# Loading a stage's weights from GpSimd's DMA queue in a hybrid attention and state space kernel

## The chip, the cores and the metric

The kernel runs on one core of a Trainium2 chip. The metric is the device time of one execution in microseconds. TensorE (PE) multiplies, VectorE (DVE) and ScalarE (ACT) work elementwise, GpSimd (POOL) does a few small operations, and SyncE (SP) does nothing but issue DMA transfers. ScalarE issues some transfers too. Each engine works through its own row of instructions in order.

## The reference

One step of a two-layer streaming encoder for 256 new frames of one stream and 32 frames of another, 288 columns in all, with a model width of 2048. Layer 0 is attention. Layer 1, which the change touches, is a state space layer:

```
h, gate = adaln(x, c, ...)
u, z = split(h @ w_in_ssm, 2)                  # 2048 x 4096
y, state = s5_sequence(u, state, abar, bbar, c)  # diagonal complex recurrence
y = y + d * u
g = gelu(y)
glu = g * sigmoid(g @ w_glu + b_glu)
x = x + gate * ((glu * silu(z)) @ w_out_ssm)
```

The recurrence has 128 groups of 16 channels with a complex state of 64 each. All values are float32.

## The kernel before, in words

Activations lie transposed, channels on partitions, as 16 tiles of 128 x 288. A weight matrix is cut into jobs: one job is one load of 1 MB (128 x 4 x 512) and the matmuls on it. To keep float32 precision, ScalarE rounds each quarter of a weight tile to `hi`, VectorE computes `lo` = w - hi, and TensorE multiplies hi and lo with a likewise split activation (`ah`, `al`): three matmuls, called a triple here, for each 128 x 128 block. One job has 16 triples. `w_in_ssm` has 32 jobs: the first 16 make u in four groups of four tiles, the other 16 make z.

Weight tiles lie in slots. `pump` (line 391) loads the next job's weights as soon as a slot is free, and a slot is free when the last `lo` of its tile is done. There are four slots; in the state space stage one of them is given to UL, so three serve the weights. The loads are written on SyncE, so a load whose slot is not free yet waits there, and all that is behind it in SyncE's row waits too.

The recurrence is side work beside the main stream, written by Python generators:

- `state_in` (line 1612): when a group of four u tiles is finished, it writes them to HBM (`ud<-MX`, one DMA) and reads them back with time steps on partitions (`MX<-ud`, eight DMAs, short pieces). Then TensorE makes `xin_ps` for each tile with weights that ScalarE loads.
- `lags` (line 1592): reads lagged copies of u (`UL<-ud`, four DMAs for a tile) into two buffers in turn.
- `inside` (line 1728): `t_ps` from UL and a small weight `kb`; then VectorE adds it to u. When t_ps is through, its UL buffer is free for the tile after next.
- `scan` (line 1651): VectorE's recurrence over 32 steps, 16 columns of two groups at a time.
- `slices` (line 1693): ScalarE arranges the states in `Xm`, TensorE makes `y_ps` with a loaded `v`; after four tiles the result goes to HBM (`yd<-Yg`, eight DMAs, short pieces).
- `gelus` (line 1750): reads it back (`yx<-yd`), adds it and applies GELU; `act_split` then makes the chunks of g.

A batch below is one round of this for four tiles; there are four.

The order of all this is fixed when the program is built. `Plan` keeps a time for each engine, `Engine.cost` (line 134) adds a cost for each instruction, and a generator goes on when the plan says that what it waits for is there. For a DMA from SyncE or GpSimd the plan has one common clock, `p.at["dma"]`, on which transfers queue one after the other. For a DMA from ScalarE it has a fixed latency and twice the size, without a queue. The written order of each engine comes from these numbers; what happens on the chip is decided by semaphores. Nearly all instructions go through line 116, so the profile is read by tiles and not by lines.

`rstd1` in `ready` marks the point early in layer 1 at which the norm of its input is there.

Of the kernel before, what the change touches and what calls it, by code (L numbers as in the profile page):

```python
# [38 lines left out]
class Plan:  # L39
# [35 lines left out]
    def run(self, eng, cost, outs, ins):  # L75
        t = self.at[eng]
        for a in ins:
            t = max(t, self.when(self.written, a) + self.LINK[eng])
        for a in outs:
            t = max(t, self.base.get(a.tensor.name, 0.0), self.when(self.read, a))  # L80
            if eng != "pe":
                t = max(t, self.when(self.written, a))
        self.at[eng] = t + cost
        end = t + cost + (0.07 if eng == "pe" else 0.0)
        for a in ins:
            self.note(self.read, a, end)
        for a in outs:
            self.note(self.written, a, end)
        self.last = max(self.last, end)
        return end  # L90
# [5 lines left out]
class Engine:  # L96
# [38 lines left out]
    def cost(self, fn, out, ins, outs, k):  # L135
        p = self.plan
        n = 1
        for d in out.shape[1:]:
            n *= d
        if fn == "dma_start":  # L140
            t = max([p.when(p.written, a) for a in ins] + [p.at[self.name], p.base.get(out.tensor.name, 0.0)])
            p.at[self.name] = t + (0.45 if self.name != "pool" else 1.0)
            size = self.pieces(out, ins[0])
            if self.name == "act":
                end = t + 3.2 + 2 * size
            else:
                p.at["dma"] = max(p.at["dma"], t + 1.2) + size
                end = p.at["dma"] + 2.0
            p.note(p.written, out, end)
            for a in ins:  # L150
                p.note(p.read, a, end)
            p.last = max(p.last, end)
            return
        if self.name == "pe":
            r = ins[1] if len(ins) > 1 else ins[0]
            w = 1
            for d in r.shape[1:]:
                w *= d
            m = out.shape[0]
            c = 0.107 if fn != "matmul" else w * 0.00042 + 0.01 if r.dtype == F32R else max(w * 0.00042, 0.024) if m <= 32 \  # L160
                else max(w * 0.00168, m * 0.00167)
            c += 0.003
        elif self.name == "act":
            c = n * 0.000833 + 0.1 + (0.1 if len(outs) > 1 else 0)
        elif self.name == "dve":
            if fn == "tensor_reduce":
                n = ins[0].shape[1] * (ins[0].shape[2] if len(ins[0].shape) > 2 else 1)
            c = 0.07 + n * (0.0063 if fn == "reciprocal" else 0.00055 if fn in ("tensor_copy", "memset") or fn == "tensor_scalar" and len(ins) < 2 else 0.00105)
        else:
            c = 0.14 + n * (0.166 if k.get("op") == ALU.pow else 0.0009 if fn == "tensor_scalar" else 0.0021)  # L170
        p.run(self.name, c, outs, ins)
# [100 lines left out]
def build(tc, I, O):  # L272
    nc = tc.nc
    plan = Plan()
    pe, act, dve, pool, sp = (Engine(e, n, plan) for e, n in (
        (nc.tensor, "pe"), (nc.scalar, "act"), (nc.vector, "dve"), (nc.gpsimd, "pool"), (nc.sync, "sp")))
# [4 lines left out]
    with ExitStack() as ctx:  # L281
# [12 lines left out]
        ready = Keys(plan)  # L294
# [88 lines left out]


        jobs = []
        st_of = {}
        pos = dict(load=0, run=0)
        st_free, slot_of, taken = list(range(NST)), {}, []
        more = dict(tiles={}, until=0)

        def pump():
            while pos["load"] < len(jobs):
                k = pos["load"]
                j = jobs[k]
                if j["kind"] == "fn":
                    j["fn"]()
                else:
                    free = [s for s in st_free if s < NST or k < more["until"]]
                    if not free:
                        break  # L400
                    slot_of[k] = free[-1] if free[-1] >= NST else free[0]
                    st_free.remove(slot_of[k])
                    t = more["tiles"][slot_of[k]]() if slot_of[k] >= NST else \
                        wst.tile([128, 4, 512], F32, tag="w%d" % slot_of[k], name="w")
                    sp.dma_start(t, j["src"])
                    st_of[k] = t
                pos["load"] += 1

# [32 lines left out]
        def rest_step(left):  # L441

            while len(rests) > left:
                k, i, st, hi, lo = rests.pop(0)
                TT(lo, st[:, i, :], hi.bitcast(F32), ALU.subtract)
                if i == 3:
                    st_done(k)
                    pump()
# [28 lines left out]
        def run_jobs(upto, n_side):  # L477
            while pos["run"] < upto:
                t = pos["run"]
                j = jobs[t]  # L480
                pump()
                if j.get("before"):
                    j["before"]()
# [942 lines left out]


        pump()
        side.add(x_stats())
        side.add(params())  # L1430
# [351 lines left out]
        for gi in range(4):  # L1782
            g = new_group(z1_evac(gi))
            for c in range(4):
                jobs.append(main_job("w_in_ssm", 4 + gi, c, g, "h1"))
                if gi == 3:
                    jobs[-1]["key"] = ("free", "h1", c)
        l1b = len(jobs)

        def glu_evac(gi):  # L1790
            def ev(n, ps, c):
# [225 lines left out]
```

## Time and profile before

| what | value |
|---|---|
| median of 3 runs | 1371.33 us (1369.74 to 1377.06) |
| the profiled execution | 1372.13 us |
| its span, first to last instruction | 1369.6 us |
| PE busy | 1237.1 us, 90% |
| DVE busy | 922.6 us, 67% |
| ACT busy | 593.4 us, 43% |
| POOL busy | 32.6 us |
| HBM read and written | 307.13 MB and 35.95 MB, 250 GB/s over the span |
| mean granted clock of TensorE | 0.960 |

The state space layer's w_in_ssm and recurrence lie from about 740 to 1145 us; the side work of the recurrence begins at about 800 us. PE's busy share is high because matmuls overlap in the records, so the time is read from the idle stretches and from what ended them. "x <-DMA y" behind a PE row names the transfer whose landing ended the wait.

### The profile page before, as it was taken

How to read it: one execution, taken by the hardware profiler on the slowest of the kernel's cores; microseconds unless marked ns; L12 is line 12 of the kernel's file. 1: busy time of each engine (PE TensorE's matmuls, PEld its weight loads, DVE VectorE, ACT ScalarE, POOL GpSimd, SP SyncE). 2: the span in 40 equal slices, each digit the busy share in tenths (PEclk: the TensorE clock that was granted, in tenths of full speed). 3: DMA queues.
4: the chain of work that ended last, by engine and by line, in shares of the span. 5: the costliest groups of instructions: out<-in, count | busy, mean ns of one | idle time of the engine just before them, and what ended most of it. 6: DMA issues, size and time to landing. Idle time of an engine off the chain costs nothing.

```text
span 1369.6 us, 28062 instructions
## 1 busy us (share of the span) xinstructions
PE 1237.1 (90%) x11098; PEld 1098.7 (80%) x11098; DVE 922.6 (67%) x2210; ACT 593.4 (43%) x1394; POOL 32.6 (2%) x21
## 2 busy tenths in 40 slices
PE   5999899999898999998899997875997998999996
PEld 3788798888787878886789896764986998989895
DVE  4579978788777877884556953745944965455454
ACT  4533233343454454454443743321553484444341
POOL 0006000000000000000000000000000000000000
PEclk9999999999999999999899998987988999999998
DMA  9978676688878878878665697989499366777631
GB/s 360 372 299 321 233 283 252 232 289 327 308 277 292 314 270 305 308 251 337 231 251 182 210 298 201 236 218 222 150 186 254 132 200 243 262 263 264 245 124 70
DMA packets 125442, 344.90 MB, mean 252 GB/s; under 512 B 50784, under 2 KB 75376, under 8 KB 94592
## 3 DMA queue, kind: packets, MB, share of 16 engines
q1 hardware_dynamic: 112640, 313.47, 67.9%
q10 hardware_dynamic: 12672, 29.65, 5.9%
q8 instruction: 87, 1.43, 0.4%
q14 instruction: 43, 0.35, 0.1%
HBM read 307.13 MB, written 35.95 MB: 250 GB/s over the span
## 4 chain that ended last, share of the span: by engine, by line
issue 44%; PE 32%; DVE 11%; DMA 10%; ACT 2%; POOL 0%; ACTq 0%; SPq 0%; DVEq 0%; POOLq 0%
PE m L116 24%; PE mod_ps L116 4%; DMA w<-in_w_in_att 4%; DVE lo L116 2%; DMA w_d<-W 2%; DMA v_d<-v 2%; DVE v L116 2%; DVE MX L116 1%; DVE tmpv L116 1%; ACT hi L116 1%; PE w_ps L116 1%; DVE qkv L116 1%; DVE dtmp L116 1%; DMA Fb<-Fp_d 1%; DVE ssq L116 1%
## 5 line engine op out<-in xcount | busy, mean ns | idle before, releaser
L116 PE MATMUL m<-ah,hi 128*128 128x288 f32 (+1 forms) x2304 | 714.6, 310 | 13.3 <-ACT hi L116 4.8
L116 PE MATMUL m<-ah,lo 128*128 128x288 f32 (+1 forms) x2304 | 689.8, 299 | 4.3 <-DVE lo L116 4.3
L116 PE MATMUL m<-al,hi 128*128 128x288 f32 (+1 forms) x2304 | 690.7, 300 | 0.4 <-DVE al L116 0.4
L116 PEld LDWEIGHTS m<-ah,hi 128*128 128x128 f32 x2304 | 443.0, 192 | 69.7 <-issue 32.3
L116 DVE TENSOR_TENSOR lo<-w,hi 128x512 fp32r<-128x512 f32 x552 | 368.4, 686 | 169.0 <-ACT hi L116 164.5
L116 ACT CAST hi<-w 128x512 fp32r<-128x512 f32 x552 | 322.0, 617 | 325.0 <-PE m L116 203.3
L116 PEld LDWEIGHTS m<-ah,lo 128*128 128x128 f32 x2304 | 443.2, 192 | 6.2 <-DVE lo L116 6.1
L116 PEld LDWEIGHTS m<-al,hi 128*128 128x128 f32 x2304 | 443.6, 193 | 1.0 <-DVE al L116 0.8
L116 PE MATMUL mod_ps<-w,cs 128*32 128x512 f32 x744 | 97.6, 619 | 12.6 <-DVE ssq L116 12.6
L116 DVE SCALAR_TENSOR_TENSOR qkv<-m,qkv 128x288 f32<-128x288 f32 x168 | 73.0, 452 | 25.9 <-PE m L116 25.7
L116 DVE TENSOR_TENSOR X<-X,t 128x32 f32<-128x32 f32 (+1 forms) x256 | 58.3, 228 | 8.2
L116 DVE TENSOR_TENSOR v<-pt,raw 128x512 f32<-128x512 f32 (+1 forms) x64 | 46.0, 718 | 13.5 <-DMA v_d<-v 13.4
L116 DVE SCALAR_TENSOR_TENSOR MX<-MX,c_dT,t_ps 128x288 f32<-128x288 f32 x16 | 8.2, 512 | 68.5 <-PE t_ps L116 68.5
L116 PE MATMUL t_ps<-UL,kb 128*32 128x288 f32 (+1 forms) x256 | 18.8, 420 | 38.4 <-DMA UL<-ud 38.4
L116 DVE SCALAR_TENSOR_TENSOR MX<-m,gate,MX 128x256 f32<-128x256 f32 x96 | 30.8, 363 | 32.2 <-PE m L116 32.1
L116 PEld LDWEIGHTS mod_ps<-w,cs 128*32 128x32 f32 x744 | 17.2, 110 | 38.0 <-issue 22.2
L116 DVE TENSOR_TENSOR tmpv<-pt,raw 128x512 f32<-128x512 f32 (+1 forms) x64 | 45.9, 718 | 0.0
L116 PEld LDWEIGHTS t_ps<-UL,kb 128*32 128x32 f32 x256 | 8.4, 124 | 46.1 <-issue 42.7
L116 PE MATMUL y_ps<-Xm,v 128*128 128x74 f32 x256 | 34.7, 294 | 10.4 <-DMA v<-v_d 5.3
L116 PEld LDWEIGHTS y_ps<-Xm,v 128*128 128x128 f32 x256 | 33.4, 210 | 11.4 <-ACT Xm L116 6.0
L116 ACT ACTIVATE yx<-MX 128x288 f32<-128x288 f32 (+1 forms) x38 | 18.8, 495 | 50.7 <-DVE MX L116 50.2
L116 DVE TENSOR_TENSOR v<-v,tmpv 128x512 f32<-128x512 f32 (+1 forms) x48 | 34.3, 714 | 1.7
(226 smaller groups left out, 910.6 us busy)
## 6 DMA issues: line engine op xcount, KB each, us to landing
w<-in_w_mod SPq DMA_DIRECT2D x93, 1024.0 KB, 6.2
w<-in_w_in_att SPq DMA_DIRECT2D x40, 1024.0 KB, 7.5
w<-in_w_in_ssm SPq DMA_DIRECT2D x32, 1024.0 KB, 6.7
w<-in_w_wide SPq DMA_DIRECT2D x24, 1024.0 KB, 10.1
w<-in_w_out_att SPq DMA_DIRECT2D x16, 1024.0 KB, 7.0
w<-in_w_glu SPq DMA_DIRECT2D x14, 1024.0 KB, 6.8
w<-in_w_out_ssm SPq DMA_DIRECT2D x12, 1024.0 KB, 5.2
v_d<-v ACTq DMA_DIRECT2D x16, 576.0 KB, 8.3
```

The lines of the kernel that those rows point to most:

```text
L116: return f(*a, **k)
```

## The change

Weight loads of the jobs up to the end of w_in_ssm (`l1b`) that are written after `rstd1` is ready are issued from GpSimd's queue. All others stay on SyncE. In the plan, a DMA from GpSimd gets the formula that ScalarE's had, so the common clock is SyncE's alone.

```
-            if self.name == "act":
-                end = t + 3.2 + 2 * size
-            else:
+            if self.name == "sp":
                 p.at["dma"] = max(p.at["dma"], t + 1.2) + size
                 end = p.at["dma"] + 2.0
+            else:
+                end = t + 3.2 + 2 * size
...
         jobs = []
+        ends = {}
...
         def pump():
+            side_end = ends.get("l1b", 0)
...
-                    sp.dma_start(t, j["src"])
+                    (pool if "rstd1" in ready and k < side_end else sp).dma_start(t, j["src"])
...
-        l1b = len(jobs)
+        l1b = ends["l1b"] = len(jobs)
```

Since the plan's times change, the written order of the other engines changes as well. On SyncE at the start of the first batch, the order before has these rows (ud and MX<-ud are the write and the read back of u, UL the lagged copies in their two buffers, kb the small weights of t_ps, x1d a copy of x in HBM):

```order
L116 DMA w<-in_w_in_ssm 128x2048 x2
L116 DMA ud<-MX 128x4x288
L116 DMA w<-in_w_in_ssm 128x2048
L116 DMA MX<-ud 16x32x36 x8
L116 DMA UL<-ud 32x4x288 x4
L116 DMA UL_9942<-ud 32x4x288 x4
L116 DMA w<-in_w_in_ssm 128x2048 x2
L116 DMA kb<-kb_d 128x256
L116 DMA UL<-ud 32x4x288 x4
L116 DMA kb<-kb_d 128x256
L116 DMA UL_9942<-ud 32x4x288 x4
```

The same place has these rows now:

```order
L116 DMA x1d<-MX 128x1152 x2
L116 DMA ud<-MX 128x4x288
L116 DMA MX<-ud 16x32x36 x8
L116 DMA UL<-ud 32x4x288 x4
L116 DMA UL_9942<-ud 32x4x288 x4
L116 DMA kb<-kb_d 128x256
L116 DMA UL<-ud 32x4x288 x4
L116 DMA kb<-kb_d 128x256
L116 DMA UL_9942<-ud 32x4x288 x4
L116 DMA kb<-kb_d 128x256 x2
```

The weight loads ahead of ud, of MX<-ud and of the third set of UL are gone from SyncE's row; the rest keeps its sequence.

In the third batch SyncE has this order before (v are the weights of y_ps, yd the write of its result):

```order
L116 DMA UL<-ud 32x4x288 x4
L116 DMA v_11330<-v_d 128x1152
L116 DMA w<-in_w_in_ssm 128x2048
L116 DMA kb<-kb_d 128x256
L116 DMA UL_9942<-ud 32x4x288 x4
L116 DMA v_11391<-v_d 128x1152
L116 DMA yd<-Yg 16x32x36 x8
L116 DMA w<-in_w_in_ssm 128x2048
L116 DMA kb<-kb_d 128x256
L116 DMA UL<-ud 32x4x288 x4
```

And this one now:

```order
L116 DMA v_11374<-v_d 128x1152
L116 DMA MX<-ud 16x32x36 x8
L116 DMA UL<-ud 32x4x288 x4
L116 DMA UL_9942<-ud 32x4x288 x4
L116 DMA v_11443<-v_d 128x1152
L116 DMA yd<-Yg 16x32x36 x8
L116 DMA kb<-kb_d 128x256
L116 DMA UL<-ud 32x4x288 x4
L116 DMA kb<-kb_d 128x256
L116 DMA UL_9942<-ud 32x4x288 x4
```

The weights are gone here too, and the eight yd stand between the second and the third set of UL as before. GpSimd's row ends with these operations now (Xm is cleared by a memset; nrm is the small operation of a norm, the last one that of the final norm):

```order
L116 MEMSET SZ 128x1728
L116 MEMSET Xm 128x592
L116 TENSOR_TENSOR nrm<-nrm,mhalf 128x3
L116 DMA w<-in_w_in_ssm 128x2048 x26
L116 TENSOR_TENSOR nrm<-nrm,mhalf 128x3
```

Before, the two nrm stood next to each other; the 26 loads are what came between them.

In TensorE's order the instructions are the same in number. Counted in triples of w_in_ssm from its start, the first xin_ps of the four batches stood at 114, 184, 226 and 356 and stand at 106, 170, 236 and 300; a group of four u tiles ends at 64, 128, 192 and 256. In a batch xin_ps and t_ps now mostly alternate with two triples between one and the next. The last y_ps stood at 500 and stands at 416, and w_in_ssm ends at 512. Everything behind w_in_ssm has the order that it had.

## The prediction

> **What bounds the kernel now.** I read the page's granted clock by slices, then a table of windows over the state space stage, then TensorE's waits in it, then SyncE's issues in order of time, and last the DMA issues with their time to landing. The page first: the profiled execution has a span of 1369.6 us.
>
> ```profile
> PEclk9999999999999999999899998987988999999998
> ```
>
> The clock sags only between slices 24 and 31, which is the state space stage. The windows cut that stretch, 800 to 1145 us, into five parts (length, busy us of PE, PEld, DVE, ACT, POOL with their counts, clock, DMA share, GB/s).
>
> ```profile
> 800.00:848.00 48.00, 37.38 (x386) 33.29 (x385) 15.52 (x31) 17.09 (x45) 0.00 (x0) 0.89 0.84 224
> 848.00:905.00 57.00, 49.49 (x492) 46.16 (x491) 42.95 (x156) 23.47 (x61) 0.00 (x0) 0.97 0.93 234
> 905.00:959.00 54.00, 30.73 (x338) 26.36 (x331) 24.69 (x96) 9.27 (x26) 0.00 (x0) 0.81 0.88 205
> 959.00:1054.00 95.00, 80.96 (x681) 76.22 (x680) 54.97 (x165) 42.23 (x109) 0.00 (x0) 0.89 0.76 196
> 1054.00:1145.00 91.00, 83.34 (x627) 82.24 (x623) 71.34 (x188) 56.64 (x138) 0.00 (x0) 1.00 0.60 193
> ```
>
> TensorE is busy 37.4 + 49.5 + 30.7 + 81.0 + 83.3 = 281.9 of the stage's 345 us, so it idles 63.1 us there. Work done below the full clock comes on top: (1 - clock) x busy gives 4.1 + 1.5 + 5.8 + 8.9 = 20.3 us at most. I take 14 us, since part of that busy time is not bound by the array. So about 77 us of this stage can be gained. The waits of TensorE from 790 to 1160 us tell who owns the idle part (total us, times, longest).
>
> ```profile
> PE t_ps L116 <- DMA UL<-ud: 38.4, 9, 13.5
> PE y_ps L116 <- DMA v<-v_d: 5.3, 1, 5.3
> PE y_ps L116 <- ACT Xm L116: 5.1, 3, 2.3
> PE m L116 <- ACT ah L116: 3.6, 1, 3.6
> PE xin_ps L116 <- DMA UL<-ud: 3.6, 2, 2.0
> PE m L116 <- DVE lo L116: 2.7, 2, 1.4
> PE xin_ps L116 <- DMA MX<-ud: 2.4, 1, 2.4
> PE xin_ps L116 <- DMA SZ<-w_d: 2.1, 1, 2.1
> ```
>
> They add up to 63.2 us, and 38.4 of it is one wait: the lagged copies UL of u, which t_ps multiplies. The issues of SyncE show why they are late (start, length, xcount; one row can hold a block in its middle).
>
> ```profile
> 802.99 1.17 SPq L116 DMA_DIRECT2D ud<-MX  x1
> ...
> 816.88 4.86 SPq L116 DMA_DIRECT2D UL<-ud  x8
> 822.07 8.29 SPq L116 DMA_DIRECT2D w<-in_w_in_ssm  x2
> 830.44 0.51 SPq L116 DMA_DIRECT2D kb<-kb_d  x1
> 831.00 2.94 SPq L116 DMA_DIRECT2D UL<-ud  x4
> ...
> 859.85 6.28 SPq L116 DMA_DIRECT2D MX<-ud  x8
> ...
> 927.11 11.75 SPq L116 DMA_DIRECT2D yd<-Yg  x8
> 938.96 0.75 SPq L116 DMA_DIRECT2D w<-in_w_in_ssm  x1
> 939.81 0.42 SPq L116 DMA_DIRECT2D kb<-kb_d  x1
> 940.28 3.08 SPq L116 DMA_DIRECT2D UL<-ud  x4
> ```
>
> At 822.07 SyncE stands for 8.29 us between two weight loads, because the second waits for a slot, and the third set of UL is behind it. TensorE's timeline has the waits that end the two sets quoted, and the three first waits of a batch.
>
> ```profile
> 821.18 1.03 PE L116 MATMUL xin_ps<-MX,W1r 128*64 128x36 f32 x29 [2.03 <-DMA UL<-ud]
> 841.68 0.71 PE L116 MATMUL t_ps<-UL,kb 128*32 128x288 f32 x4 [8.57 <-DMA UL<-ud]
> 872.04 1.13 PE L116 MATMUL xin_ps<-MX,SZ 128*64 128x36 f32 x32 [2.39 <-DMA MX<-ud]
> 913.56 0.66 PE L116 MATMUL xin_ps<-MX,SZ 128*64 128x36 f32 x16 [1.53 <-DMA UL<-ud]
> 952.62 0.71 PE L116 MATMUL t_ps<-UL,kb 128*32 128x288 f32 x4 [13.54 <-DMA UL<-ud]
> ```
>
> **The change part by part.** Two things change: 26 weight loads leave SyncE's row for GpSimd's, and the planner, which now believes that UL, MX and yd do not queue behind weights, writes another order. Two rows of the main stream give its pace, the first and the last of 75 rows in a row.
>
> ```profile
> 859.46 0.29 PE L116 MATMUL m<-ah,hi 128*128 128x290 f32 x1
> 869.36 0.29 PE L116 MATMUL m<-ah,lo 128*128 128x290 f32 x1
> ```
>
> That is 9.90 / 74 = 0.134 us a matmul, 0.40 us for a triple, the unit of the order. The side work of the stage has these groups (busy us, mean ns, idle before), and the DMAs these landing times from 800 to 1145 us (median us).
>
> ```profile
> L116 PE MATMUL t_ps<-UL,kb 128*32 128x288 f32 (+1 forms) x256 | 18.8, 420 | 38.4 <-DMA UL<-ud 38.4
> L116 PE MATMUL y_ps<-Xm,v 128*128 128x74 f32 x256 | 34.7, 294 | 10.4 <-DMA v<-v_d 5.3 <-ACT Xm L116 5.1
> ```
>
> ```profile
> w<-in_w_in_ssm SPq DMA_DIRECT2D x24, 1024.0 KB, 7.0
> UL<-ud SPq DMA_DIRECT2D x64, 144.0 KB, 6.7
> ud<-MX SPq DMA_DIRECT2D x4, 576.0 KB, 7.5
> MX<-ud SPq DMA_DIRECT2D x32, 72.0 KB, 5.3
> ```
>
> *UL within a batch.* There are two UL buffers, so the third set can be asked for only when the first t_ps is through. Its time then is four issues (2.94 us in the row at 831.00) and the landing of the last (6.7): 9.6 us. In the new order TensorE has, between the end of that t_ps and the one that needs the set, two xin_ps (1.13 each, row 872.04), one t_ps (18.8 / 16 = 1.2) and eight triples (3.2): 6.7 us. So a batch still waits 3 us, and the fourth set, asked for while the third lands, nothing. In the last two batches eight yd writes still stand ahead of the third set; in the row at 927.11 they hold SyncE 11.75 us, of which I take 4 us as wait. Sum 4 x 3 + 2 x 4 = 20 us in place of 38.4: 18.4 gained. The ends are 8 us, if the last issue lands in the 5.3 us that MX takes and the yd cost 1 us a batch, and 32 us (the rival below).
>
> *The front of a batch.* From the end of a group of four tiles to the first xin_ps lie 50, 56, 34 and 100 triples in the old order and 42, 42, 44 and 44 in the new one, counted in TensorE's order. The chain that has to fit is the finish of u, then ud, MX and its landing. In batch 0 it takes 2.03 + 50 x 0.40 = 22 us, of which 18.2 lie between ud's issue at 802.99 and xin_ps at 821.18, and I leave it at that. Batch 0 then waits 2.03 + 8 x 0.40 = 5 us. Batch 1 waits 2.39 + 14 x 0.40 = 8, less about 2 for the weights that no longer stand ahead of ud and of MX: 6. In batches 2 and 3 four y_ps (34.7 / 16 = 2.2 each) lie between as well, so TensorE has 44 x 0.40 + 8.7 = 26 us of work for the 22 of the chain; loads of v, which wait for y_ps, stand ahead of MX there, and I take 2 us each, from 0 to 5. Sum 15 in place of the 6.0 of the two xin_ps rows on UL and MX: 9 lost.
>
> *The smaller waits.* The wait of y_ps for v (5.3) I put at 0, since v no longer shares SyncE's row with weights that wait. The wait for ah (3.6) comes at the stage's end, where the last y_ps stood 12 triples before the end of w_in_ssm and now stand 96 before it, 38 us of cover: 0. Xm, lo and SZ (9.9) stay. Together 8.9 gained, and without that cover nothing.
>
> *The clock.* Idle goes from 63.2 to 20 + 15 + 9.9 = 44.9 us, and the waits of 8.6 and 13.5 us are the ones that shrink most. I scale the 14 us of clock loss to half: 7 gained; the bounds are 0 and 14.
>
> *The loads on GpSimd.* No DMA of the program runs from GpSimd before, so its price is bounded by rows: nothing, or the longest thing that GpSimd does for a small operand.
>
> ```profile
> L116 POOL TENSOR_TENSOR nrm<-nrm,mhalf 128x3 f32<-128x3 f32 x3 | 2.5, 850 | 651.7 <-DVE nrm L116 651.7
> ```
>
> I take 1 us more of landing, 8 for 7.0. The cover is the slot's cycle: three weight slots serve this stage, and a slot is held for its load and for the four splits that go at the pace of one job, 16 x 0.40 = 6.4 us. (8 + 6.4) / 3 = 4.8 us a job, under 6.4: hidden. Behind the waiting loads on GpSimd stand only later loads and the last nrm, which needs the end of the kernel. The planner's different landing time only chooses the order.
>
> Sum: 18.4 - 9 + 8.9 + 7 = 25.3 us off 1372.13, the profiled execution's own time, so 1346.8. That execution lies 0.8 above the median of 1371.33, which makes 1346 us. With the ends of the terms (UL 8 to 30, front 9 to 22, clock 0 to 12) the case's own range is 1328 to 1362.
>
> **The rivals.** *More goes.* If the UL sets land at the lower end, their waits are 8 us, so 12 more are gained, and with fewer long waits another 7 of clock: 1327. Against it stand the DMA shares of 0.84 to 0.93 up to 905 us.
>
> *The DMA engines are the bound.* The same bytes go through the same 16 engines, and the new order asks for them in fewer microseconds. By the rows, UL took 10.7 us (831.00 to 841.68) and 12.3 (940.28 to 952.62) from first issue to use; at 12.5 a batch waits 6, with the yd 32 in all. The fronts at 6 to 8 make 26, so idle is 32 + 26 + 10 = 68 us, the clock as now, and the smaller gains are eaten: 1371, within 8. The rows with share 0.93 and idle TensorE speak for it, the 8.29 us of SyncE standing still against it. [...]
>
> *Slower: the weights come late.* In the last third of the stage the main stream runs nearly alone. If a load from GpSimd takes L, a job takes (L + 6.4) / 3; that passes 6.4 us at L = 12.8, and each microsecond beyond costs 26 / 3 = 8.7 us. The 25 us are eaten at about L = 16, and at L = 18 the time is 1346 + 45 = 1391; I put the case at 1388. For it: lo already makes m wait 2.7 us, so slots are tight. Against it: L is 7.0 on SyncE. [...]
>
> **How the numbers follow.** The forecast has 0.48, "more goes" 0.12, the DMA bound 0.22, the late weights 0.18. The range 1325 to 1378 leaves out about 0.05 below and 0.13 above. Half a per cent is 7 us, about what a measurement of this kernel can tell. Faster by over that is the forecast but for 0.02, "more goes", and 0.06 of the DMA bound: 0.64. Slower is the late weights and 0.03 of the DMA bound: 0.21. Within it: 0.15.
>
> **What would show it.** Right: the stage from 800 us is about 25 us shorter; t_ps waits for UL 20 us or so in place of 38.4; xin_ps waits more than now, 15 us; no wait of SyncE among UL for a weight slot; the ah wait is gone; loads on GpSimd land in 7 to 9 us. Wrong: UL from first issue to use still above 11 us (then the engines bind), or waits of ACT hi for w in_w_in_ssm and landing above 13 us (then the weights bind).

## The result and the profile after

The changed kernel takes 1389.12 us (median of 4 runs, 1386.69 to 1390.81), the kernel before in the same comparison 1374.19 us (4 runs, 1369.74 to 1377.41). The ratio is 1.011, with a 95% interval from 1.007 to 1.0149: slower by about 1%, where 25 us or 1.8% faster was predicted. The profiled execution took 1386.69 us, with a span of 1384.9.

The page's row of granted clock, in 40 slices, now falls to 7 and 6 in the state space stage, where its lowest digit was 7:

```profile
PEclk9999999999999999998999999897969999999998
```

To compare equal work, I cut both traces at the same two places of the main stream: 64 triples after the start of w_in_ssm and 64 triples after its end, which holds all four batches. In the window of the kernel before the columns are length, then busy us and count of PE, PEld, DVE, ACT and POOL, then clock, DMA share and GB/s:

```profile
798.90:1155.50 356.60, 293.05 (x2570) 274.24 (x2568) 215.21 (x644) 153.30 (x388) 0.00 (x0) 0.91 0.76 204
```

The same stretch of the changed kernel:

```profile
801.80:1170.20 368.40, 303.59 (x2571) 280.58 (x2569) 214.21 (x644) 153.21 (x388) 12.96 (x24) 0.87 0.73 199
```

The stretch is 11.8 us longer, nearly all of the loss: it starts 2.9 us later, at a place that the change does not reach, and 0.6 us comes behind it. TensorE's idle time, length less busy, is 63.6 us before and 64.8 after. So the sum of the waits did not change. What grew is the busy time of the same matmuls, 293.05 to 303.59, by 10.5 us, at a mean clock of 0.87 in place of 0.91. By the clock records of the two traces TensorE was busy at half clock for 40.2 us of the stretch before and for 65.4 after; half of the 25.2 us between them is 12.6, near the 10.5.

The waits of TensorE from 790 to 1190 us (total us, times, longest) show that the idle time has other owners now. "issue" is a wait for which the profile has no releaser; the one of 6.4 us ends at 1018.80, just behind the landing of its UL set's last transfer at 1018.60, so it is one more wait for UL.

```profile
PE t_ps L116 <- DMA UL<-ud: 36.2, 6, 13.9
PE xin_ps L116 <- DMA UL<-ud: 12.2, 2, 6.5
PE t_ps L116 <- issue: 6.4, 1, 6.4
PE y_ps L116 <- ACT Xm L116: 5.6, 5, 2.0
PE xin_ps L116 <- DMA MX<-ud: 3.7, 1, 3.7
PE xin_ps L116 <- issue: 0.6, 1, 0.6
```

In the code xin_ps multiplies MX and its own weights and never reads UL. By the records of the two traces MX and UL count on the same eight semaphores (see the last section), and such a row names the transfer that counted last: the wait that ends at 824.60 is put down to UL, and the last MX had landed at 824.51. So all rows of xin_ps are read here as waits of the front.

The waits for v, for ah, for lo and for SZ are gone. The t_ps waits are 42.6 us with the one under "issue", against 38.4 before. TensorE's timeline has them one by one (start, length of the 16 matmuls, the wait ahead in brackets):

```profile
824.60 1.93 PE L116 MATMUL xin_ps<-MX,W1r 128*64 128x36 f32 x32 [5.74 <-DMA UL<-ud]
839.51 1.44 PE L116 MATMUL t_ps<-UL,kb 128*32 128x288 f32 x16 [2.74 <-DMA UL<-ud]
846.93 1.67 PE L116 MATMUL t_ps<-UL,kb 128*32 128x288 f32 x16 [1.94 <-DMA UL<-ud]
...
881.68 1.67 PE L116 MATMUL t_ps<-UL,kb 128*32 128x288 f32 x16 [9.41 <-DMA UL<-ud]
902.71 1.67 PE L116 MATMUL t_ps<-UL,kb 128*32 128x288 f32 x16 [5.13 <-DMA UL<-ud]
940.81 1.93 PE L116 MATMUL xin_ps<-MX,SZ 128*64 128x36 f32 x32 [6.50 <-DMA UL<-ud]
966.78 1.67 PE L116 MATMUL t_ps<-UL,kb 128*32 128x288 f32 x16 [13.88 <-DMA UL<-ud]
1008.73 1.93 PE L116 MATMUL xin_ps<-MX,W1r 128*64 128x36 f32 x32 [3.65 <-DMA MX<-ud]
1018.80 1.67 PE L116 MATMUL t_ps<-UL,kb 128*32 128x288 f32 x16 [6.40 <-issue]
1035.47 1.67 PE L116 MATMUL t_ps<-UL,kb 128*32 128x288 f32 x16 [3.06 <-DMA UL<-ud]
```

Two things are to be seen. By sets, the first t_ps of batches 1 and 3 wait 9.41 and 6.40, the third ones 2.74, 13.88 and 3.06, and the fourth ones of batches 0 and 1 1.94 and 5.13. And the length of the 16 matmuls tells the clock: 1.67 us behind six of these seven waits, 1.44 behind the other. The granted clock is 0.50 from 881.68 to 883.40, where one of the 1.67 lies, and 1.00 from 1025.00 to 1026.00 in the kernel before, where one of 0.94 lies. These are six of the nine t_ps rows of the kernel before that stand behind a wait; four of them, behind short waits, take 0.94 us, the other two 1.67:

```profile
876.31 0.94 PE L116 MATMUL t_ps<-UL,kb 128*32 128x288 f32 x16 [2.15 <-DMA UL<-ud]
...
922.90 1.67 PE L116 MATMUL t_ps<-UL,kb 128*32 128x288 f32 x16 [7.21 <-DMA UL<-ud]
931.06 0.94 PE L116 MATMUL t_ps<-UL,kb 128*32 128x288 f32 x16 [0.98 <-DMA UL<-ud]
952.62 1.67 PE L116 MATMUL t_ps<-UL,kb 128*32 128x288 f32 x16 [13.54 <-DMA UL<-ud]
1025.13 0.94 PE L116 MATMUL t_ps<-UL,kb 128*32 128x288 f32 x16 [1.58 <-DMA UL<-ud]
1048.38 0.94 PE L116 MATMUL t_ps<-UL,kb 128*32 128x288 f32 x16 [1.51 <-DMA UL<-ud]
```

SyncE's issues around the two longest t_ps waits (start, length of the block, count):

```profile
865.52 12.80 SPq L116 DMA_DIRECT2D UL<-ud  x8
...
948.62 10.48 SPq L116 DMA_DIRECT2D yd<-Yg  x8
959.20 0.59 SPq L116 DMA_DIRECT2D kb<-kb_d  x1
959.83 2.74 SPq L116 DMA_DIRECT2D UL<-ud  x4
```

The first two sets of batch 1 take 12.80 us to issue, though no weight of w_in_ssm is in SyncE's row. In batch 2 eight yd hold the row for 10.48 us ahead of the third set. What SyncE waits for from 790 to 1190 us explains the 12.80:

```profile
SPq L116 <- DMA SZ<-w_d: 25.2, 6, 6.0
SPq L116 <- DMA W1r<-w_d: 20.3, 4, 8.4
```

SyncE moves nothing that needs W1r, and SZ<-w_d is a load of the same kind: both are the weights of xin_ps, loaded by ScalarE. So SyncE waits for landings of another engine's transfers with which it shares no data. In batch 1 it stands 8.4 us for one W1r, which ScalarE issued at 868.65 and which landed at 875.00; SyncE's next UL goes out at 875.02. The kernel before has such waits too, 22.2 and 17.8 us in the same window, 40.0 for 45.5 now. The weights themselves are in time; their median landing from GpSimd is 7.3 us:

```profile
w<-in_w_in_ssm POOLq DMA_DIRECT2D x24, 1024.0 KB, 7.3
UL<-ud SPq DMA_DIRECT2D x64, 144.0 KB, 6.0
```

### The profile page after: what moved, and what is told of

It reads as the page before. It is cut to its first block, busy times and chain, and to the rows that moved or that the text cites. A ratio compares the mean times of both kernels' runs of the same rounds, so it can differ in the third digit from the quotient of the medians.

```text
span 1384.9 us, 28092 instructions
## 1 busy us (share of the span) xinstructions
PE 1245.7 (90%) x11098; PEld 1102.5 (80%) x11098; DVE 921.5 (67%) x2210; ACT 593.2 (43%) x1394; POOL 46.9 (3%) x47
## 4 chain that ended last, share of the span: by engine, by line
PE 37%; issue 25%; DMA 21%; DVE 10%; SPq 3%; ACT 3%; POOL 0%; ACTq 0%; DVEq 0%; POOLq 0%
PE m L116 27%; DMA w<-in_w_in_att 5%; PE mod_ps L116 4%; DMA UL<-ud 3%; SPq L116 3%; DMA w_d<-W 3%; DVE lo L116 2%; DMA v_d<-v 2%; DVE v L116 2%; DMA w<-in_w_out_att 1%; PE y_ps L116 1%; DMA yd<-Yg 1%; ACT hi L116 1%; DMA SZ<-w_d 1%; DMA W1r<-w_d 1%
## 5 line engine op out<-in xcount | busy, mean ns | idle before, releaser
L116 PE MATMUL t_ps<-UL,kb 128*32 128x288 f32 (+1 forms) x256 | 23.3, 504 | 42.6 <-DMA UL<-ud 36.2
L116 PEld LDWEIGHTS mod_ps<-w,cs 128*32 128x32 f32 x744 | 17.2, 110 | 37.9 <-issue 22.2
L116 PE MATMUL w_ps<-c_ident,v 128*128 128x128 f32 x128 | 21.0, 288 | 19.5 <-DVE v L116 6.9
L116 PEld LDWEIGHTS w_ps<-c_ident,v 128*128 128x128 f32 x128 | 14.9, 145 | 27.8 <-issue 8.9
L116 PE MATMUL y_ps<-Xm,v 128*128 128x74 f32 x256 | 31.7, 278 | 5.8 <-ACT Xm L116 5.6
```

Of the source, the lines that this page charges most:

```text
L116: return f(*a, **k)
```

## The experiments

Theory 1: the written order is what costs; the planner now takes UL, MX and yd to be there too early, puts their users too close behind them, and TensorE waits and falls to half clock. Theory 2: the queue costs. Below, "the stretch" is that of equal work as above, and the table at the end has it for all runs.

**The queue alone, and the order alone.** The change was parted in two. The kernel before, with its order, has its 26 loads issued by GpSimd while the planner reckons them as SyncE's:

```
-                    sp.dma_start(t, j["src"])
+                    sp.cost("dma_start", t, [j["src"]], [t], {})
+                    (pool if "rstd1" in ready and k < ends.get("l1b", 0) else sp).eng.dma_start(t, j["src"])
```

> The order of every engine is that of the kernel before; only the 26 weight loads go to GpSimd's queue. Theory 1 (the written order is what costs, the queue helps): t_ps waits for UL fall from 38 us to 20 to 28, the fronts of the batches stay at 4 to 8, and the time is 8 to 20 us under the kernel before, ratio 0.985 to 0.994. Theory 2 (the queue itself costs, by slower loads or by weights that take the engines from UL): waits for UL stay at 36 us or more and the ratio is 1.005 or above. Theory 3 (nothing but issue time goes): ratio 0.997 to 1.003.

It took 1368.78 us, ratio 0.996 (0.9935 to 0.9984), between theories 1 and 3. The third set of batch 0, behind the weight load that stood for a slot, now waits 1.05 us where it waited 8.57, as the prediction reads it. But the t_ps waits for UL are 30.4, not 20 to 28, and the first xin_ps of batch 2 waits 12.09 where it waited 1.53: most of what the queue frees comes back at other places. The other half is the changed kernel's order with the loads issued by SyncE:

```
-                    (pool if "rstd1" in ready and k < side_end else sp).dma_start(t, j["src"])
+                    (pool if "rstd1" in ready and k < side_end else sp).cost("dma_start", t, [j["src"]], [t], {})
+                    sp.eng.dma_start(t, j["src"])
```

> The order of every engine is that of the changed kernel, and all weight loads are back on SyncE at the place in the program where GpSimd had them. Theory 1: a tight order with weights in SyncE's row is the worst of both, ratio 1.015 to 1.035, t_ps waits above 45 us. Theory 2: without the queue the loss goes, ratio 0.99 to 1.003. Theory 3: as the changed kernel, ratio 1.008 to 1.014.

It took 1399.48 us, ratio 1.0191 (1.0157 to 1.0226), as theory 1 said, though with t_ps waits of 41.3 us and not above 45. So the queue is worth 4 us in the old order and 10 in the new one (1399.5 to 1389.1), and the new order costs 20 us with the queue (1368.8 to 1389.1) and 27 without. Theory 2, that the queue costs, falls.

**The loads of ScalarE.** They stand where SyncE waits, so 13 of the 16 were left out of the changed kernel:

```
-                act.dma_start(b, w1_d[k])
+                act.cost("dma_start", b, [w1_d[k]], [b], {})
+                if k < 3:
+                    act.eng.dma_start(b, w1_d[k])
```

> The changed kernel in the same order, but ScalarE issues only 3 of the 16 loads of xin_ps's weights (512 KB each), so 13 are left out and xin_ps multiplies old ones. Theory 1a (SyncE's transfers wait for the landing of the transfer issued eight before them, and that is often one of these loads): SyncE no longer waits for SZ or W1r loads (now 25 and 20 us), UL sets are issued without the stalls of 7 to 9 us, and TensorE's waits for UL in t_ps and xin_ps fall from 55 to about 25 us, the span by 20 to 30 us. Theory 3a (only bytes count): 13 x 0.5 MB less of 72 MB in the stage is 9 per cent, so waits fall by 5 us and the span by about as much.

One run took 1364.83 us, 24 less than the changed kernel. That fits the theory that these loads hold SyncE, but it also takes 6.5 MB out of the stage. So the same was left out of the kernel before:

> The kernel before, with its order, and 13 of the 16 loads of xin_ps weights left out: the control for the run that left them out of the changed kernel (22 to 24 us less). Theory 1a in its strong form (it is the new order that brings these loads in the way): the kernel before gains little, 0 to 8 us, so 1364 to 1372. Rival (these loads cost the same in either order, by bytes or by turn, and so are not what the change made worse): 1345 to 1354, and the changed kernel stays 15 us or so behind.

With the same edit there it took 1343.26 us, ratio 0.9782 (0.9755 to 0.9809), 30 us less. Loads and bytes together cost at least as much in the old order, so they are not what the change made worse. The third run of this group keeps all bytes of the changed kernel and takes the loads out of ScalarE's row:

```
-                act.dma_start(b, w1_d[k])
+                act.cost("dma_start", b, [w1_d[k]], [b], {})
+                pool.eng.dma_start(b, w1_d[k])
```

> The changed kernel, its order and all its bytes, with the 16 loads of xin_ps weights (512 KB each) issued by GpSimd in place of ScalarE; nothing is left out. It parts the two readings of the run that left 13 of them out and took 22 to 24 us less than the changed kernel. Theory 1a (these loads stand in the turn of completion semaphores that SyncE's transfers wait for): SyncE's 45 us of waits on SZ and W1r go and the time is 1368 to 1380. Rival, bytes (the loads only took DMA time): 1385 to 1392, as changed. Third case: the loads stand on GpSimd behind weights that wait for slots, xin_ps then waits 10 us or more for W1r and SZ, and the time is over 1392.

It took 1376.61 us (10 runs, 1371.07 to 1383.82), ratio to before 1.0024 (1.0001 to 1.0048), 12 us less than the changed kernel and inside theory 1a's range; its profiled execution, 1383.82 us, is the longest of the ten, so its trace shows less than this gain. SyncE's waits for SZ and W1r are gone from its list, and the first two sets of batch 1 issue in less than half the time:

```profile
867.79 5.08 SPq L116 DMA_DIRECT2D UL<-ud  x8
```

But in this execution the waits of TensorE did not go; they moved to other sets.

```profile
PE t_ps L116 <- DMA UL<-ud: 38.7, 6, 10.3
PE xin_ps L116 <- DMA UL<-ud: 15.0, 2, 8.9
```

The first t_ps of batch 1 waits 2.94 where it waited 9.41, and the third 7.85 where it waited nothing:

```profile
878.03 1.64 PE L116 MATMUL t_ps<-UL,kb 128*32 128x288 f32 x16 [2.94 <-DMA UL<-ud]
896.42 1.67 PE L116 MATMUL t_ps<-UL,kb 128*32 128x288 f32 x16 [7.85 <-DMA UL<-ud]
```

Its idle time in the stretch is 65.5 us, as in the changed kernel (64.8); what it gains there is 4.7 us of busy time. The hold on SyncE is real, and without it this order is 12 us faster; with it gone the sets land later (7.4 us in the median for 6.0). It does not explain the loss by itself: the kernel before has 40.0 us of it, leaving out 13 loads gained more there than here (30 and 24 us), and the order shown next has 47.4 us of it (40.6 for SZ, 6.8 for W1r) and takes 1344.58 us. What moving the loads would bring in the order before was not measured.

**More cover in the order.** If the sets are asked for too close ahead of their use, it should help to tell the planner that they land later. That moves nothing to another queue and adds no byte; the batches start later and the users of a set stand farther behind it:

```
-                end = p.at["dma"] + 2.0
+                end = p.at["dma"] + 2.0 + p.extra
...
             ready.add("rstd1")
+            plan.extra = 4.0
```

`extra` is 0 outside the stage. With 4 us the batches start at triples 126, 194, 240 and 312 in place of 106, 170, 236 and 300, and the last y_ps stands at 446 in place of 416.

> The changed kernel, but the plan believes that transfers from SyncE land 4 us later in this stage, so xin_ps and t_ps stand further apart (first xin_ps at triples 126, 194, 240, 312 and not 106, 170, 236, 300). Theory 1: waits for UL fall to 20 to 30 us in all, the stretches at half clock get shorter, and the time is 10 to 25 us under the changed kernel, ratio to the kernel before 0.99 to 1.003. Theory 2: as the changed kernel within 4 us. Theory 3: within 4 us as well, the wait only moves.

It took 1344.58 us, ratio 0.9787 (0.9749 to 0.9824): more than theory 1 asked for, and faster than both kernels. Its waits:

```profile
PE t_ps L117 <- DMA UL<-ud: 21.6, 6, 7.0
PE y_ps L117 <- ACT Xm L117: 7.0, 4, 2.6
PE xin_ps L117 <- DMA UL<-ud: 3.2, 1, 3.2
PE xin_ps L117 <- DMA MX<-ud: 2.6, 1, 2.6
```

The t_ps waits are half of the 42.6, the xin_ps waits 6.5 for 16.5, with 0.7 for W1r further down in this view. The stretch:

```profile
805.30:1128.90 323.60, 287.15 (x2570) 269.70 (x2568) 214.19 (x644) 152.89 (x388) 12.90 (x24) 0.93 0.83 227
```

Idle is 36.5 us and busy 287.15. It moves the bytes of the stretch in 45 us less than the changed kernel, at 227 GB/s for 199 and a DMA share of 0.83 for 0.73, so the 16 DMA engines were not full before. The same edit with 2 us and with 8 us gives the dose:

> The changed kernel with 2 us more of landing for SyncE's transfers of the stage in the planner, between 0 (1389.1), 4 (1344.6) and 8 (1345.9). If cover for the landing is what decides, it lies between the first two, 1360 to 1372, with t_ps waits of about 30 us. If the gain of 4 us was the luck of one order, it lies anywhere, also at 1375 or more.

> The changed kernel with 8 us more of landing for SyncE's transfers of the stage in the planner, where 4 us gave 1344.6. The batches then start at triples 146, 222, 298 and 386 in place of 126, 194, 240 and 312, and the last y_ps stands at 510 of 576. Theory 1 (a tight order is what makes TensorE wait and run at half clock): the 21.6 us of t_ps on UL fall under 12, the half-rate time of 44 under 35, and the time is 1330 to 1341. Rival (4 us were enough, and the tail of the side work now comes near the end of the stage): waits of the last batch and of what follows eat it, 1343 to 1358.

With 2 us it took 1362.15, ratio 0.9919 (0.9891 to 0.9947); with 8 us 1345.89, ratio 0.9798 (0.9773 to 0.9823). From 0 to 4 us the time falls as cover grows, 1389.1, 1362.2, 1344.6, and then no more; the expectation of 1330 to 1341 for 8 us failed, and the rival's did not. The t_ps waits did fall to 11.0 there, but the first xin_ps of the third and of the last batch now wait 11.42 and 10.29. The wait of the last batch, and 4.6 at the end of the stage, are what the rival meant; that of the third is not. With 2 us, 1360 to 1372 and waits of about 30 were expected, and 1362.15 and 27.4 came. That an order is lucky by itself can't be ruled out for one point; three points in a row speak for the cover. They are three different orders, not one that is stretched: with 2 us the fourth batch starts at triple 330, later than the 300 and 312 of its neighbours. (In the second text 576 is the end of the counted stretch; w_in_ssm ends at 512.) The queue's part under the order of 4 us was measured with the loads on SyncE again, by the edit of the order alone:

> The order of the version with 4 us more of landing in the planner, word for word, with the 26 weight loads issued by SyncE again. That version took 1344.6 us with the loads on GpSimd. Theory 1 (the order carries the time and the queue is a small separate gain): with the old order the queue was worth 4 us, with the tight one 10, so 1348 to 1357. Theory 2 (the later order pays only since SyncE's row is free of waiting weights): it falls back to the kernel before, 1366 to 1376. Theory 3 (the queue is worth nothing here): 1342 to 1347.

It took 1358.9 us, ratio 0.9892 (0.9865 to 0.9918). The queue is worth 14 us here; the time lies 1.9 us above theory 1's range and below theory 2's. With the sets covered, the weight loads in SyncE's row are in their way: from 790 to 1190 us they (line 409 of that run) stand 80.4 us, 19 times, for the last lo of a slot. Last, the 4 us were given to the transfers of UL alone, in `lags`:

```
-            plan.extra = 4.0
+            plan.extra = 0.0
...
                 UL[n] = ul_free.pop(0).rearrange("p (g t) -> p g t", g=4)
+                plan.extra = 4.0
                 for l in range(4):
...
                 ready.add(("ul", n))
+                plan.extra = 0.0
```

> The changed kernel with 4 us more of landing in the planner for the transfers of UL alone; ud, MX, yd, v and kb keep their times, and the batches start at 106, 168, 220 and 336 as the changed kernel's do in the first two. Theory 1 (the t_ps waits, 42.6 us with those behind issues, are sets of UL that the planner took to be there): t_ps waits fall to 25, the time is 1355 to 1368. Rival (the front, ud and MX, is what needs the cover): the xin_ps waits stay at 16 and the sets follow them, 1375 to 1388.

It took 1373.23 us, ratio 1.0007 (0.9988 to 1.0027), between both expectations. The t_ps waits are 20.9 for UL, as theory 1 said, but the xin_ps waits under the name of UL, which are those of the front, are 19.8:

```profile
PE t_ps L117 <- DMA UL<-ud: 20.9, 4, 7.2
PE xin_ps L117 <- DMA UL<-ud: 19.8, 3, 8.9
```

With cover for UL alone the wait stands one step up the chain, at xin_ps, whose transfers ud and MX were given none.

**The clock by itself.** Idle time was the same before and after; the loss stands in busy time. To see whether that is the clock, TensorE was kept at work in the waits: matmuls of a constant are put ahead of the nine products that wait longest in the changed kernel's trace, into the PSUM tile that the product then overwrites:

```
                 tps = take([128, T], "t_ps")
+                for _ in range({2: 8, 4: 36, 7: 18, 10: 54, 12: 24, 14: 8}.get(i, 0)):
+                    pe.eng.matmul(tps[:, 0:128], lhsT=ident, rhs=ident, start=True, stop=True, skip_group_check=True)
```

and likewise 22, 24 and 12 ahead of three xin_ps.

> The changed kernel, its order and its transfers, with matmuls of a constant (128x128, overwritten by the product that follows) put on TensorE just ahead of the nine products that wait longest in the changed kernel's trace: 58 of them ahead of three xin_ps, 148 ahead of six t_ps, as many as fill most of each wait. They bring nothing but a busy TensorE. In the trace of the changed kernel TensorE worked 65 us of the stage at half clock, before 40. Theory 1 (waits of the same sum now cost more because each is followed by work at half clock): the work at half clock falls by 25 to 35 us, of which half is time, so 1371 to 1378. Rival (the clock has little to do with it, the waits themselves are the time): 1385 to 1392. A filler too long for its wait costs up to 3 us.

It took 1381.57 us, ratio to before 1.006 (1.0043 to 1.0077), 8 us less than the changed kernel, between the two expectations: 3.6 us above theory 1's, 3.4 below the rival's. The groups of the added matmuls (busy, mean ns, idle before):

```profile
L1744 PE MATMUL t_ps<-c_ident 128*128 128x128 f32 x296 | 34.1, 275 | 0.0
L1637 PE MATMUL xin_ps<-c_ident 128*128 128x128 f32 x116 | 13.4, 275 | 0.0
```

and the stretch:

```profile
806.50:1169.30 362.80, 331.41 (x2982) 314.01 (x2981) 214.08 (x644) 153.80 (x389) 12.91 (x24) 0.96 0.74 201
```

The added work is 34.1 + 13.4 = 47.5 us, and without it TensorE is busy 331.4 - 47.5 = 283.9 us, 19.7 less than the 303.6 of the changed kernel for the same matmuls. The clock is 0.96 for 0.87, and of TensorE's busy time, added work included, 23.1 us are at half clock for 65.4. So the clock does cost that much here. Idle and added work together are 31.4 + 47.5 = 78.9 us against the 64.8 idle of the changed kernel, 14.1 more, where I had allowed 3: fillers that overshoot may be in it, and waits that differ from one execution to the next, but neither was shown. The stretch gains 19.7 - 14.1 = 5.6 us. The same in the order with 4 us (10 and 12 ahead of two xin_ps; 14, 8, 28 and 26 ahead of four t_ps) brought nothing:

> The version with 4 us more of landing in the planner (1344.6 us) with such matmuls ahead of six products that wait in its trace (22 ahead of two xin_ps, 76 ahead of four t_ps). It worked 31 us at half clock. Theory 1: about 20 of these go, half of it is time: 1332 to 1338. Rival: 1343 to 1348.

It took 1345.11 us, ratio 0.98 (0.9768 to 0.9832), as its rival said. Fillers are a way to measure the clock here, not a way to speed.

The stretch of equal work in all kernels (us; idle is length less busy; each from the one profiled execution; "fewer" leaves out 13 loads):

| kernel | time | length | PE busy | idle |
|---|---|---|---|---|
| before | 1374.2 | 356.6 | 293.1 | 63.6 |
| changed | 1389.1 | 368.4 | 303.6 | 64.8 |
| queue alone | 1368.8 | 353.5 | 291.3 | 62.2 |
| order alone | 1399.5 | 380.9 | 304.5 | 76.4 |
| changed, fewer loads | 1364.8 | 345.7 | 297.5 | 48.2 |
| before, fewer loads | 1343.3 | 322.7 | 285.8 | 36.9 |
| changed, loads on GpSimd | 1376.6 | 364.4 | 298.9 | 65.5 |
| changed, 2 us | 1362.2 | 339.3 | 296.2 | 43.1 |
| changed, 4 us | 1344.6 | 323.6 | 287.2 | 36.5 |
| changed, 8 us | 1345.9 | 325.1 | 285.7 | 39.4 |
| 4 us, loads on SyncE | 1358.9 | 342.7 | 298.1 | 44.6 |
| 4 us for UL alone | 1373.2 | 354.3 | 295.1 | 59.2 |
| changed, fillers | 1381.6 | 362.8 | 331.4 | 31.4 |
| 4 us, fillers | 1345.1 | 324.4 | 304.8 | 19.6 |

## Why the prediction was wrong, step by step

The sum promised 25.3 us less in the stage; the stretch got 11.8 longer. The 37.1 us between them lie in two terms: the waits of UL within a batch, and the clock.

*UL within a batch: the step that failed.* The prediction put all 38.4 us of t_ps waits down to third sets and let 20 stand. By the rows of the kernel before only 8.57 + 13.54 + 1.51 = 23.6 were third sets; 2.15 + 7.21 + 1.58 = 10.9 were first sets, and the rest second and fourth ones. For third sets the forecast's sum came out, 2.74 + 13.88 + 3.06 = 19.7 for 20, but by luck: batches 0 to 3 wait 2.7, 0, 13.9 and 3.1 where 3, 3, 7 and 7 were said. Since their price before was wrong, 3.9 us went there and not 18.4. First sets had no term at all: the front was worked out to the first xin_ps and no further, and behind it t_ps of batches 1 and 3 waits 9.41 + 6.40 = 15.8. Fourth sets were put at nothing and wait 7.1. That is 42.6 for 20.

*The front of a batch: right in its sum.* 15 was said, and the xin_ps waits are 12.2 + 3.7 + 0.6 = 16.5. By batches they are 5.7, 0.6, 6.5 and 3.7 where 5, 6, 2 and 2 were said, so that this sum fits is partly luck. Together with t_ps the two terms are 59.1 for 35, so 24.1 us of the miss.

*The smaller waits: right and more.* v and ah went as said; lo and SZ went too, and Xm rose by 0.5. That is 13.2 us for 8.9, so 4.3 better.

*The clock: wrong in sign.* A gain of 7 was taken, since idle would fall and the long waits shrink. Idle did not fall, and the busy time rose by 10.5: 17.5 us of the miss. The sum is 24.1 - 4.3 + 17.5 = 37.3, and 37.1 was to be explained. Why equal idle time costs more now is read from the rows and was not tested alone: it lies in fewer and longer waits, 16 for 21. Of these five were above 3.5 us before (8.57, 7.21 and 13.54 of t_ps, 5.26 of y_ps, 3.57 of m), and seven are now (9.41, 5.13, 13.88 and 6.40 of t_ps, 5.74, 6.50 and 3.65 of xin_ps). In the clock records the granted clock is 0.50 behind each of the twelve. The run with fillers shows that the clock is the price.

Short waits lower it in some places and not in others: before, t_ps ran in 0.94 us behind waits of 0.86 to 2.15, and after, in 1.67 behind one of 1.94, which comes 7 us after another of 2.74. That they stand close does not decide it, for before, waits of 2.39 and 2.15 end 4 us apart at full clock. In the stage's clock records the granted clock changes only after 3.41 us or a multiple of it (last section), and TensorE's busy time in such a step of 3.41 us does not decide it either. In the step from 874.60 of the kernel before, which holds most of the second of these waits, it is busy for 1.70 us, and the clock of the next step is 1.00. In the step from 843.21 of the changed kernel, with most of the wait of 1.94, it is busy for 1.79, and the next step has 0.50. What decides for the short ones stays open.

For the long ones the rows agree: behind all seven t_ps waits of 5.13 to 13.88 us in the two traces the 16 matmuls took 1.67 us. The 1.67 behind the wait of 1.94 shows that the length of one wait does not decide alone. (The row of granted clock by slices, from which the prediction starts, also has an 8 in slice 20 and in the last one, outside the stage; the changed kernel has them too, in slices 19 and 40.)

*The loads on GpSimd: right.* 8 us of landing was taken, 7.3 was measured, and no wait for lo is left: the rival of late weights is refuted. That its 1388 us lie beside the measured 1389 is luck.

*The rival of full DMA engines* said 68 us of idle time, and 64.8 came, so its idle time was the better one. Its time was not: 1371 was written, and its own 68 us for the 63.2 before make 1377. Its reason does not hold: with 4 us of cover the same bytes pass 45 us sooner. And its sign for "wrong", UL from first issue to use above 11 us, holds for the first set of batch 1 (865.52 to 881.68 is 16.2, of which 8.4 is the wait for W1r) and not for the third one of batch 2 (959.83 to 966.78 is 6.9). What the queue itself brings was measured: with the queue alone 4 us, in the new order 10, and with 4 us of cover 14, where SyncE's weight loads, put back, stand for slots and hold what is behind them (the 80.4 us above).

*The range* was narrower than its own ends. UL 8 to 30, front 9 to 22 and clock 0 to 12, added with the 8.9 of the smaller waits, give 1329 to 1376 and not 1328 to 1362; and the lower end of UL is 38.4 - 32 = 6.4 and not 8 by the paragraph on UL. No end of any term had the clock get worse, and that alone is 10.5 us.

*The cause.* The planner's clock for SyncE's transfers, relieved of the weights, ends a UL set 2 us after its place on that clock. The trace has 6.0 us for one transfer, and 6.9 and 16.2 for the two sets above from first issue to use. That the weights on the same clock had stood in for a landing that the planner reckons too short is a reading; the other new thing in the planner, its own formula for the weights' landing, was not tested apart. Shown is that the order made without them costs 20 us with the queue held equal, against the 4 to 10 that the queue brings, and that 4 us more of landing gives back 45.

## What to carry to other kernels

When a transfer leaves a queue and a planner sets the order, measure the two parts apart: the same order on the new queue, and the new order on the old one. A cost in the model that looks like mere contention may be the only cover that landing times have; put the measured landing in its place before the queue is changed. And price a wait by who waits, set by set, and by the clock of the work behind it: idle time can stay the same while the time grows.

## What the runs showed of the hardware

The semaphore numbers and the clock steps below are measured: they are read from the records of this case's two traces, before and after.

A transfer of SyncE waited for landings of ScalarE's transfers with which it shares no data: 45.5 us in the changed kernel, and none in the run with these loads issued by GpSimd. In the records each transfer carries the number of the semaphore that its landing counts on. The transfers of SyncE and ScalarE carry the same eight numbers (99, 101 to 105, 107 and 108), 75 or 76 transfers each in the changed kernel; GpSimd's 26 carry eight others (111 to 118). On the three of the eight whose landings are all on record there (99, 101 and 107), no transfer of the 226 went out before the one ahead of it on its semaphore had landed. The UL that went out at 875.02 and the W1r that it waited for, which landed at 875.00, both have number 105.

Issue from GpSimd cost little: its busy time rose from 32.6 to 46.9 us for 26 loads, 0.55 each.

At half clock 16 matmuls of t_ps took 1.67 us for 0.94. With 412 filler matmuls the clock of the stretch was 0.96 for 0.87, and the busy time of the stage's own matmuls was 19.7 us shorter. In the clock records of the stage, before and after, each stretch at half clock lasts 3.41 us or a multiple of it, from 3.41 to 20.48.
